# Conditioning weights in column halves, interleaved PSUM columns, the order of work at a stage seam, and a new share-out of routing one-hots in a decoder-layer kernel

## The chip, the cores and the metric

The kernel runs on one core of one Trainium2 chip. The metric is the device time of one execution in microseconds (us), taken as the median over repeated runs; lower is better. All times below are microseconds unless they are marked ns.

Engine names in the profile: PE is TensorE (PEld its weight loads), DVE is VectorE, ACT is ScalarE, POOL is GpSimd, SP is SyncE. A name with a q (SPq, ACTq, POOLq) is the instruction queue of that engine, where it issues transfers.

## The reference

One layer of a decoder on 1024 tokens of width 1024, all in float32:

```
mod = silu(c) @ ada_w + ada_b                    # (1024) @ (1024, 6144): six vectors
h   = rms_norm(x) * (1 + sc1) + sh1
... two kinds of causal attention on h, projected back ...
x   = x + g1 * (mixed @ w_out)
h2  = rms_norm(x) * (1 + sc2) + sh2
# PEER: 8 heads, 16 experts per head and token out of 128 * 128
q   = h2 @ w_q ; s = q . sub_keys                # two score lists of 128 per head
eidx, g = top-16 of the sums of the two lists' top-16, softmax
a   = gelu(u_tab[eidx] . h2)
y   = sum over the 128 chosen experts of g * a * v_tab[eidx]
x   = x + g2 * y
```

## The kernel before

The 1024 tokens are 8 tiles of 128. The program runs these stages one after another, and in each an engine takes its instructions in order:

1. **Conditioning and projections.** `ada(g, wp)` works out a third (2048 columns) of `mod`. The silu of c is repeated over 32 columns as the stationary operand, so one product fills only 32 of the 128 columns of TensorE's array, and four products for four blocks q of 512 columns can stand side by side (`tile_position=(0, 32 * q)`). For g = 0 a weight tile holds all four q (128x2048); for g = 1 and 2 it holds two of them (128x1024, contiguous rows of 4 KB), so each tile brings two products of 512 columns. These 32 tiles go through two buffers, issued by SP, and are woven into the projections (`project`), whose weights also come through SP.
2. **Attention, output projection and queries for tiles 0 to 4** (`block(0, DT)`).
3. **The same for tiles 5 to 7 (`block(DT, ...)`), woven with `route_dense`.** For each of tiles 0 to 4, `routing` finds the experts and `matrix(t)` turns them into a dense matrix of weights. It goes in 32 groups of four tokens: `A` holds for each token a one-hot row per chosen expert (VectorE, one instruction for four tokens), `B` a weighted one-hot row (one token at a time, on GpSimd, VectorE, or ScalarE, which needs two instructions, Abs and Relu). The string `SHARE[t]` says who does which of eight tokens: P, D or A. TensorE multiplies A by B, one product per token into a bank of PSUM `pg`; float32 products are two instructions each, so a group has eight. ScalarE (line 904) copies `pg` into `gs`, where the four tokens of a group lie next to each other and a row j begins every 32 elements. The copy reads PSUM in order and writes every 32nd element. Per tile this makes 128 B rows, 32 copies and 4 transfers `gd<-gs`. GpSimd also does the subtractions `wl` of the weight splits in this stage. The order on each engine in stages 1 to 3 is made by a planner that works from estimated costs.
4. **Experts** (`experts`, order written by hand). Step j of 128: `mm_u(j)`, 48 matmuls against two split tiles of the expert table, `us[2j]` and `us[2j+1]` (24 each); `gelu(j)`; `weigh(j)`, a product with the dense matrix; `split_c(j)`; and, from step 4 on, `mm_v` blocks that use `split_v` tiles. `split_u(n)` is a copy on ScalarE (high part), a subtraction (low part) on GpSimd where n < UP and else on VectorE, and the issue on SP of the load of tile n+3. `split_v(n)` is alike with VP. Between them `step()` runs a share of `gathered`: routing of tiles 5 to 7 and their gathered experts (VectorE multiplies at line 974, GpSimd issues the gathers at line 954).

The end of a step in stage 4, before:

```
if not blocks and live:          # j = 0 to 3
    for i in (j - 1, j) if j == NJ - 1 else (j - 1,):
        if i >= 0:
            weigh(i)
            if i < 2:
                split_c(i)
if jj % 2 == 1 and (g >= 0 or jj == 3):
    ...                          # two split_v
if live:
    split_u(2 * j + 3)
```

Of the kernel before, what the change touches and what calls it, by code (L numbers as in the profile page):

```python
# [24 lines left out]
P = 128  # L25
# [9 lines left out]
GB = 32  # L35
NA, NB = 3, 3
PACE = (1.3, 1.05, 1.5)
SHARE = ['PAPDPAPD', 'PAPDPAPD', 'PAPDPAPD', 'PDADPDAD', 'DDADPDAD']
NJ = 4
LAGS = 3  # L40
AHEAD = 2
PG = 2
LAGV = 2
UP, VP = 8, 8

UR, VR = 3, 4

# [38 lines left out]
def decoder_layer(ctx: ExitStack, tc: tile.TileContext, a, out):  # L86
# [8 lines left out]
    PS = {}  # L95
# [23 lines left out]
    def bank(name="pj"):  # L119
        return PS[name].tile([P, 512], FT, name=name)  # L120

    def tpt():
        return tp.tile([P, 4, P], FT, name="tp")
# [57 lines left out]
    def ada(g, wp):  # L181

        bt = wp.tile([P, 512], FT, name="abias", bufs=1)
        for q in range(4):
            o = a["ada_b"].offset + g * 2048 + q * 512
            (nc.gpsimd if g else nc.scalar).dma_start(bt[32 * q:32 * q + 32, :],
                                bass.AP(tensor=a["ada_b"].tensor, offset=o, ap=[[0, 32], [1, 512]]))
        ps = bank()
        n = 2 if g else 4
        for k in range(8):  # L190
            for q0 in range(0, 4, n):
                w = wp.tile([P, n, 512], FT, name="adaw")
                c = g * 2048 + q0 * 512
                (nc.sync if g or k % 2 == 0 else nc.scalar).dma_start(w, adaw[k, :, c:c + n * 512])
                for q in range(q0, q0 + n):
                    nc.tensor.matmul(ps[32 * q:32 * q + 32, :512], silb[:, k, :], w[:, q - q0, :], start=(k == 0),
                                     stop=(k == 7), skip_group_check=True, tile_position=(0, 32 * q))
        m = bt
        nc.vector.tensor_add(m, ps[:, :512], bt)
        for q in range(4 if g else 0):  # L200
            o = q * 512
            nc.gpsimd.dma_start(modd[2 * g + o // D, o % D:o % D + 512], m[32 * q:32 * q + 1, :])
        return m
# [661 lines left out]
    def route_dense(ts):  # L865

        with ExitStack() as c1:
            rp = pool(c1, "rp", 1)
            gp = pool(c1, "gp", 2)
            def matrix(t):  # L870
                r = R.pop(t)
                pt = tpt()
                for q in range(2):
                    nc.tensor.transpose(pt[:, q, :], r["e"][:, q, :], ident)
                nc.tensor.transpose(pt[:, 2, :], r["g"].rearrange("p h k -> p (h k)"), ident)
                T = gp.tile([P, 4, P], FT, name="T", bufs=1)
                nc.vector.tensor_copy(T[:, 0:3, :], pt[:, 0:3, :])  # L877
                nc.vector.tensor_scalar(T[:, 3, :], pt[:, 2, :], -1.0, None, op0=OP.mult)
                nj = gp.tile([P, P], FT, name="nj", bufs=1)
                nc.vector.tensor_scalar(nj, pt[:, 1, :], -1.0, None, op0=OP.mult)  # L880
                for b in range(P // GB):
                    gs = gp.tile([P, P, GB], FT, name="gs")
                    for m0 in range(0, GB, 4):
                        A = gp.tile([P, 4, P], FT, name="A", bufs=NA)
                        B = gp.tile([P, 4, P], FT, name="B", bufs=NB)
                        c = b * GB + m0
                        nc.vector.tensor_tensor(A, T[:, 0, c:c + 4, None].to_broadcast([P, 4, P]),
                                                iota128[:, None, :].to_broadcast([P, 4, P]), op=OP.is_equal)
                        for m in range(4):
                            who = SHARE[t][(m0 + m) % 8]  # L890
                            if who == "P":
                                nc.gpsimd.tensor_scalar(B[:, m, :], iota128, T[:, 1, c + m:c + m + 1],  # L892
                                                        T[:, 2, c + m:c + m + 1], op0=OP.is_equal, op1=OP.mult)
                            elif who == "A":
                                nc.scalar.activation(B[:, m, :], iota128, AF.Abs, bias=nj[:, c + m:c + m + 1])
                                nc.scalar.activation(B[:, m, :], B[:, m, :], AF.Relu, bias=T[:, 2, c + m:c + m + 1],
                                                     scale=T[:, 3, c + m:c + m + 1])
                            else:
                                nc.vector.tensor_scalar(B[:, m, :], iota128, T[:, 1, c + m:c + m + 1],
                                                        T[:, 2, c + m:c + m + 1], op0=OP.is_equal, op1=OP.mult)  # L900
                        pg = bank("pg").rearrange("p (a b) -> p a b", b=P) if "pg" in PS else tpt()
                        for o in range(4):
                            nc.tensor.matmul(pg[:, o, :], A[:, o, :], B[:, o, :], start=True, stop=True)  # L903
                        nc.scalar.activation(gs[:, :, m0:m0 + 4].rearrange("p j t -> p t j"), pg, AF.Copy)  # L904
                        yield 1.2
                    nc.scalar.dma_start(gd[:, :, t * (P // GB) + b].rearrange("p a j t -> p a (j t)"),
                                      gs.rearrange("p (a j) t -> p a (j t)", j=NJ))

            ts = list(ts)
            yield 10.0  # L910
            yield from routing(ts[0], rp)
            for t, nxt in zip(ts, ts[1:] + [None]):
                yield from weave((matrix(t), 1.0), (routing(nxt, rp) if nxt else iter(()), 0.8))
# [88 lines left out]
    def experts():  # L1002
        with ExitStack() as c1, tc.manual_schedule():
# [133 lines left out]
            for j in range(P + NJ):  # L1137
                if j == P:
                    tick(1.0)
                    fin["g2"] = rows(modd, 5 * D, D, gath.tile([P, D], FT, name="gath"), nc.sync)  # L1140
                    fin["x1"] = [gath.tile([P, D], FT, name="gath") for _ in range(DT)]
                    for i in range(DT):
                        nc.sync.dma_start(fin["x1"][i], x1d[i])
                    yr = yp.tile([P, 2, 512], FT, name="yr")
                    fin["rest"] = [yr[:, 0, :], yr[:, 1, :], gath.tile([P, D], FT, name="gath")[:, :512]]
                g, jj = j // NJ - 1, j % NJ
                blocks = [(g, c, i) for c, i in V[jj]] if g >= 0 else []
                live = j < P
                tk = [0]

                def step():
                    tk[0] += 1
                    tick((j + tk[0] / 6) / 127)

                if live:
                    ps = mm_u(j)
                if j == 0:
                    split_u(3)
                    for _ in range(10):
                        prog[0] = next(sg)  # L1160
                while pend:
                    retire()
                if jj == 0 and g >= 0:
                    split_c(j - 2)
                    split_c(j - 1)
                n0 = (2 * g + jj // 2) * NJ
                if g >= 0 and jj % 2 == 0:
                    split_v(n0 + 2)
                    split_v(n0 + 3)
                step()  # L1170
                if live:
                    split_u(2 * j + 2)
                step()
                if live:
                    gelu(j, ps)
                for b, blk in enumerate(blocks):
                    pv = mm_v(*blk)
                    if b == 0 and live:
                        weigh(j)
                        if jj < 2:  # L1180
                            split_c(j)
                    if len(pend) >= LAGV:
                        retire()
                    pend.append((*blk, pv))
                    step()
                if not blocks and live:

                    for i in (j - 1, j) if j == NJ - 1 else (j - 1,):
                        if i >= 0:
# [4 lines that stand above are left out]
                    n1 = (2 * g + jj // 2 + 1) * NJ  # L1194
                    split_v(n1)
                    split_v(n1 + 1)
                if live:
                    split_u(2 * j + 3)
                while tk[0] < 6:
                    step()  # L1200
# [92 lines left out]
```

## Time and profile before

| what | value |
|---|---|
| median of 3 runs | 3039.43 us (3036.16 to 3045.69) |
| the profiled execution | 3038.61 us, its span 3036.8 us |
| TensorE busy | 2837.1 us (93%) |
| VectorE busy | 2570.6 us (85%) |
| ScalarE busy | 1185.2 us (39%) |
| GpSimd busy | 1418.7 us (47%) |
| mean granted TensorE clock | 0.974 |

The span is the time from the first to the last instruction of the one profiled execution. Busy shares are averages over stages with different limits, so a stage has to be read by itself. TensorE's matmuls are pipelined, so that its busy time is above the time for which its array works.

### The profile page before, as it was taken

What the parts mean: (1) busy time and instruction counts of PE and PEld (TensorE: products, weight loads), DVE (VectorE), ACT (ScalarE), POOL (GpSimd) and SP (SyncE); (2) the same over time, 40 slices, a digit from 0 to 9 for tenths busy, and PEclk for the clock granted to TensorE, in tenths of its full rate; (3) what the DMA queues carried; (4) which work ended last, traced back from release to release, by engine and by line L of the source; (5) the groups of instructions that cost most, each with busy time, mean ns of one, the idle gap of its engine ahead of it and who ended that gap; (6) DMA issues with size and microseconds to landing.
All of it is one profiled execution on the core that took longest, in us unless ns stands there. A gap on an engine that the chain in (4) does not pass through costs nothing.

```text
span 3036.8 us, 46727 instructions
## 1 busy us (share of the span) xinstructions
PE 2837.1 (93%) x16323; PEld 2526.6 (83%) x16323; DVE 2570.6 (85%) x5380; ACT 1185.2 (39%) x2371; POOL 1418.7 (47%) x1194
## 2 busy tenths in 40 slices
PE   5999989897888799699999999999999999999998
PEld 3678777796776698699999999999989989998887
DVE  3767366599988899788888999999999999989997
ACT  4554375242886898222322222222222222222221
POOL 1121000000669974343444655566656666655761
PEclk9999999998999899899999999999999999999999
DMA  7664464721445664678798999899999999998995
GB/s 269 201 190 123 134 199 148 277 64 56 126 129 180 210 206 140 224 263 276 255 321 310 321 332 327 319 351 368 361 351 365 358 371 359 361 373 312 365 366 200
DMA packets 375564, 794.22 MB, mean 262 GB/s; under 512 B 31392, under 2 KB 171040, under 8 KB 368672
## 3 DMA queue, kind: packets, MB, share of 16 engines
q0 software_dynamic: 114400, 417.15, 38.3%
q1 hardware_dynamic: 153344, 312.48, 29.5%
q10 hardware_dynamic: 107584, 61.61, 6.9%
q8 instruction: 128, 2.10, 0.3%
q14 instruction: 108, 0.88, 0.1%
HBM read 707.74 MB, written 83.38 MB: 261 GB/s over the span
## 4 chain that ended last, share of the span: by engine, by line
PE 49%; DVE 18%; issue 12%; POOL 7%; DMA 6%; ACT 4%; SPq 0%; DVEq 0%; POOLq 0%; ACTq 0%
PE mm L1063 14%; PE pj L288 4%; PE pj L289 4%; PE pj L290 4%; POOL gath L954 4%; DVE yr L987 4%; DVE gath L974 3%; PE pg L903 3%; PE tp L289 2%; PE tp L290 2%; PE tp L288 2%; POOL B L892 2%; PE acc L288 1%; PE acc L289 1%; PE acc L290 1%
## 5 line engine op out<-in xcount | busy, mean ns | idle before, releaser
L1063 PE MATMUL mm<-h2d,uh 128*128 128x320 f32 x4096 | 770.6, 310 | 10.2 <-ACT C L1070 5.1
L954 POOL DMA_INDIRECT gath<-in_peer_u,ei x384 | 485.5, 1264 | 405.3 <-DVE gath L974 269.4
L1063 PEld LDWEIGHTS mm<-h2d,uh 128*128 128x128 f32 x4096 | 649.7, 189 | 21.1 <-ACT C L1070 6.2
L954 POOL DMA_INDIRECT gath<-in_peer_v,ef x384 | 514.9, 1341 | 307.2 <-DVE yr L987 168.7
L987 DVE SCALAR_TENSOR_TENSOR yr<-gath,co,yr 128x1024 f32<-128x1024 f32 x381 | 487.5, 1280 | 5.5 <-DMA gath<-in_peer_v,ef 1.1
L974 DVE SCALAR_TENSOR_TENSOR gath<-gath,h 128x1024 f32<-128x1024 f32 x384 | 462.7, 1221 | 26.0 <-DMA h<-h2d 13.4
L1063 PE MATMUL mm<-h2d,ul 128*128 128x320 f32 x2048 | 471.2, 311 | 12.9 <-DVE ul L279 12.4
L1070 ACT ACTIVATE C<-mm 128x640 f32<-128x640 f32 x128 | 90.5, 707 | 864.1 <-PE mm L1063 859.0
L892 POOL TENSOR_SCALAR B<-iota,T 128x128 f32<-128x128 f32 x240 | 265.6, 1115 | 266.5 <-DVE T L877 200.7
L1063 PEld LDWEIGHTS mm<-h2d,ul 128*128 128x128 f32 x2048 | 343.0, 188 | 18.3 <-DVE ul L279 17.9
L289 PE MATMUL tp<-vl,CH 128*128 128x512 f32 x600 | 235.6, 393 | 14.8 <-POOL vl L279 11.7
L903 PE MATMUL pg<-B,A 128*128 128x128 f32 x1280 | 197.2, 298 | 48.2 <-POOL B L892 26.8
L278 ACT ACTIVATE vh<-vr 128x512 fp32r<-128x512 f32 x256 | 152.9, 622 | 224.0 <-PE tp L290 145.5
L288 PE MATMUL tp<-vh,CH 128*128 128x512 f32 x600 | 234.6, 391 | 0.0
L290 PE MATMUL tp<-vh,CL 128*128 128x512 f32 x600 | 234.1, 390 | 0.0
L903 PEld LDWEIGHTS pg<-B,A 128*128 128x128 f32 x1280 | 174.9, 206 | 69.0 <-POOL B L892 39.3
L904 ACT ACTIVATE gs<-pg 128x512 f32<-128x512 f32 x160 | 173.8, 1087 | 56.7 <-PE pg L903 56.2
L278 ACT ACTIVATE uh<-ur 128x512 fp32r<-128x512 f32 x256 | 155.4, 619 | 74.8 <-DMA ur<-in_u_t 67.7
L279 DVE TENSOR_TENSOR ul<-ur,uh 128x512 fp32r<-128x512 f32 x248 | 173.6, 700 | 0.0
L279 DVE TENSOR_TENSOR vl<-vr,vh 128x512 fp32r<-128x512 f32 x248 | 160.0, 682 | 7.2 <-ACT vh L278 7.0
L1074 DVE TENSOR_TENSOR C<-C,G 128x640 f32<-128x640 f32 x128 | 105.2, 823 | 55.0 <-ACT C L1070 54.9
L288 PE MATMUL acc<-vh,CH 128*128 128x512 f32 x384 | 149.8, 390 | 0.0
(321 smaller groups left out, 5978.9 us busy)
## 6 DMA issues: line engine op xcount, KB each, us to landing
ur<-in_u_t SPq DMA_DIRECT2D x256, 256.0 KB, 6.3
vr<-in_peer_v SPq DMA_DIRECT2D x256, 256.0 KB, 6.9
gd<-gs ACTq DMA_DIRECT2D x20, 2048.0 KB, 9.3
G<-gd SPq DMA_DIRECT2D x32, 1280.0 KB, 8.8
adaw<-in_ada_w SPq DMA_DIRECT2D x32, 512.0 KB, 4.3
wraw<-in_peer_w_q SPq DMA_DIRECT2D x128, 128.0 KB, 2.7
wraw<-in_w_out SPq DMA_DIRECT2D x32, 256.0 KB, 3.6
wraw<-in_w_in SPq DMA_DIRECT2D x24, 256.0 KB, 3.8
```

The lines of the kernel that those rows point to most:

```text
L278: nc.scalar.activation(hi, src, AF.Copy)
L279: (eng or nc.vector).tensor_sub(lo, src, hi.bitcast(FT))
L288: nc.tensor.matmul(out, ah, bh, start=start, stop=False)
L289: nc.tensor.matmul(out, ah, bl, start=False, stop=False)
L290: nc.tensor.matmul(out, al, bh, start=False, stop=stop)
L892: nc.gpsimd.tensor_scalar(B[:, m, :], iota128, T[:, 1, c + m:c + m + 1], T[:, 2, c + m:c + m + 1], op0=OP.is_equal, op1=OP.mult)
L903: nc.tensor.matmul(pg[:, o, :], A[:, o, :], B[:, o, :], start=True, stop=True)
L904: nc.scalar.activation(gs[:, :, m0:m0 + 4].rearrange("p j t -> p t j"), pg, AF.Copy)
L954: nc.gpsimd.indirect_dma_start(out=u, out_offset=None, in_=tab, in_offset=bass.IndirectOffsetOnAxis(ap=idx, axis=0))
L974: nc.vector.scalar_tensor_tensor(got[n], got[n], 1.0, q["h2"], op0=OP.mult, op1=OP.mult, accum_out=q["dots"][:, s:s + 1])
L987: nc.vector.scalar_tensor_tensor(yr, v, q["co"][:, s:s + 1], yr, op0=OP.mult, op1=OP.add)
L1063: nc.tensor.matmul(ps[:, o, 0:C2], s[:, k % 4, :], h2[:, mv, k, o * C2:(o + 1) * C2], start=st, stop=(k == 7 and s is l))
```

## The change

Four things are edited.

- In `ada`, for g = 1 and 2, a weight tile holds 256 columns of each of the four blocks q instead of 512 columns of two of them. There are as many tiles of as many bytes. Each brings four products of 256 columns, side by side, into one of two PSUM banks (one per half of the columns); a row of a tile is four pieces of 1 KB. The bias is added in two halves. g = 0 keeps its sizes.
- In `matrix`, the product of token o goes to every fourth column of `pg`, so that `pg` is laid out (row j, token t). ScalarE's copy then reads PSUM in order and writes four neighbouring elements, then the next four 32 elements on.
- `SHARE`: per eight tokens one P becomes an A in tiles 0 to 2, and one D becomes an A in tiles 3 and 4: 80 rows B in all (48 off GpSimd, 32 off VectorE).
- In `experts`, `split_u(2j+3)` goes ahead of `weigh` and `split_c` in steps 1 to 3, `split_u(3)` goes from behind `mm_u(0)` to behind `gelu(0)`, and VP is 0, so that the subtractions of the first eight `split_v` go from GpSimd to VectorE.

```
-SHARE = ['PAPDPAPD', 'PAPDPAPD', 'PAPDPAPD', 'PDADPDAD', 'DDADPDAD']
+SHARE = ['PAADPAPD', 'PAADPAPD', 'PAADPAPD', 'PAADPDAD', 'DAADPDAD']
...
-UP, VP = 8, 8
+UP, VP = 8, 0
...
-        ps = bank()
-        n = 2 if g else 4
+
+        H = 256 if g else 512
+        pss = [bank() for _ in range(0, 512, H)]
         for k in range(8):
-            for q0 in range(0, 4, n):
-                w = wp.tile([P, n, 512], FT, name="adaw")
-                c = g * 2048 + q0 * 512
-                (nc.sync if g or k % 2 == 0 else nc.scalar).dma_start(w, adaw[k, :, c:c + n * 512])
-                for q in range(q0, q0 + n):
-                    nc.tensor.matmul(ps[32 * q:32 * q + 32, :512], silb[:, k, :], w[:, q - q0, :], start=(k == 0),
-                                     stop=(k == 7), skip_group_check=True, tile_position=(0, 32 * q))
+            for h0 in range(0, 512, H):
+                w = wp.tile([P, 4, H], FT, name="adaw")
+                src = adaw[k, :, g * 2048:(g + 1) * 2048].rearrange("p (q n) -> p q n", n=512)[:, :, h0:h0 + H]
+                (nc.sync if g or k % 2 == 0 else nc.scalar).dma_start(w, src)
+                for q in range(4):
+                    nc.tensor.matmul(pss[h0 // H][32 * q:32 * q + 32, :H], silb[:, k, :], w[:, q, :],
+                                     start=(k == 0), stop=(k == 7), skip_group_check=True, tile_position=(0, 32 * q))
         m = bt
-        nc.vector.tensor_add(m, ps[:, :512], bt)
+        for i, ps in enumerate(pss):
+            nc.vector.tensor_add(m[:, i * H:(i + 1) * H], ps[:, :H], bt[:, i * H:(i + 1) * H])
...
-                        pg = bank("pg").rearrange("p (a b) -> p a b", b=P) if "pg" in PS else tpt()
+
+                        pg = (bank("pg") if "pg" in PS else tpt().rearrange("p a b -> p (a b)")).rearrange(
+                            "p (j t) -> p j t", t=4)
                         for o in range(4):
-                            nc.tensor.matmul(pg[:, o, :], A[:, o, :], B[:, o, :], start=True, stop=True)
-                        nc.scalar.activation(gs[:, :, m0:m0 + 4].rearrange("p j t -> p t j"), pg, AF.Copy)
+                            nc.tensor.matmul(pg[:, :, o], A[:, o, :], B[:, o, :], start=True, stop=True)
+                        nc.scalar.activation(gs[:, :, m0:m0 + 4], pg, AF.Copy)
...
                 if j == 0:
-                    split_u(3)
                     for _ in range(10):
                         prog[0] = next(sg)
...
                 if not blocks and live:
+                    split_u(2 * j + 3)
 
                     for i in (j - 1, j) if j == NJ - 1 else (j - 1,):
```

## Rows read from the trace of the kernel before

**Rows 1.** The page's first part: busy us, share of the span, instructions.

```profile
span 3036.8 us, 46727 instructions
PE 2837.1 (93%) x16323; PEld 2526.6 (83%) x16323; DVE 2570.6 (85%) x5380; ACT 1185.2 (39%) x2371; POOL 1418.7 (47%) x1194
```

**Rows 2.** Busy time by stretch, one for each tile of `matrix`; clock, DMA share, GB/s last.

```profile
761.00:876.00 115.00, 101.67 (x717) 91.92 (x716) 101.72 (x278) 95.55 (x187) 74.96 (x70) 0.91 0.39 121
876.00:980.00 104.00, 82.98 (x498) 71.70 (x497) 92.33 (x227) 77.61 (x143) 93.41 (x78) 0.90 0.53 162
980.00:1064.00 84.00, 64.33 (x376) 54.93 (x374) 69.79 (x132) 66.51 (x128) 84.00 (x74) 0.90 0.67 217
1064.00:1135.00 71.00, 67.57 (x470) 65.36 (x471) 67.12 (x249) 65.36 (x143) 58.11 (x65) 0.98 0.66 201
1135.00:1213.00 78.00, 72.86 (x512) 68.91 (x510) 78.00 (x331) 64.52 (x139) 36.08 (x41) 1.00 0.50 146
```

**Rows 3.** The chain that ended last, 980 to 1064 us, shares by line.

```profile
by line: POOL B L892 50.7%; issue 13.1%; PE pg L903 11.4%; POOL wl L279 4.6%; PE pj L289 3.4%; PE pj L288 3.0%; PE pj L290 3.0%; DVE B L899 2.9%; ACT B L895 1.7%; DVE A L887 1.7%; ACT B L896 1.1%; PE tp L739 1.1%; ACT mH L278 0.7%; DVE T L8
```

**Rows 4.** Groups by form, 760 to 1215 us, and one of the page: busy us, mean ns | idle before.

```profile
L892 POOL TENSOR_SCALAR B<-iota,T 128x128 f32<-128x128 f32 x240 | 265.6, 1115 | 266.5 <-DVE T L877 200.7 <-PE pg L903 44.4 <-ACT B L896 5.1
...
L904 ACT ACTIVATE gs<-pg 128x512 f32<-128x512 f32 x160 | 173.8, 1087 | 56.7 <-PE pg L903 56.2 <-ACT sc L782 0.2
...
L899 DVE TENSOR_SCALAR B<-iota,T 128x128 f32<-128x128 f32 x240 | 92.9, 413 | 0.0
L896 ACT ACTIVATE B<-B,T 128x128 f32<-128x128 f32 x160 | 78.6, 495 | 7.6 <-ACT B L895 3.7 <-DMA h2d<-h2td 2.0 <-ACT sc L782 0.2
L895 ACT ACTIVATE B<-iota,nj 128x128 f32<-128x128 f32 x160 | 59.5, 374 | 0.6 <-DVE nj L880 0.6
...
L593 ACT ACTIVATE pT<-tp 128x512 f32<-128x512 f32 x26 | 15.6, 603 | 1.7 <-PE tp L592 1.7
...
L279 DVE TENSOR_TENSOR vl<-vr,vh 128x512 fp32r<-128x512 f32 x248 | 160.0, 682 | 7.2 <-ACT vh L278 7.0
```

**Rows 5.** The chain in order of time: start, us, what.

```profile
1110.51 0.90 PE pg L903 x8
...
1279.92 7.04 PE mm L1063 x48
```

**Rows 6.** Timeline of TensorE, conditioning: weight loads for g = 0, a tile for g = 1.

```profile
35.58 0.12 PEld L196 LDWEIGHTS pj<-adaw,silb 128*32 128x32 f32 x4 [0.31 <-issue]
36.01 0.12 PEld L196 LDWEIGHTS pj<-adaw,silb 128*32 128x32 f32 x4 [0.31 <-issue]
...
96.20 1.05 PE L196 MATMUL pj<-adaw,silb 128*32 128x512 f32 x4
97.19 0.45 PE L290 MATMUL pj<-wh,hL 128*128 128x384 f32 x1
```

**Rows 7.** The chain that ended last, 46 to 193 us, shares by line.

```profile
by line: PE pj L288 6.7%; DMA qd<-stage 6.6%; PE pj L289 6.0%; PE pj L290 5.9%; DMA wraw<-in_w_in 5.7%; PE pj L196 4.7%; DMA adaw<-in_ada_w 4.3%; PE tp L452 1.7%; issue 1.2%; ACT hf L367 1.1%; DVE stage L284 1.0%; DVE hf L370 0.8%; ACT hH L
```

**Rows 8.** Transfers: KB each, median us from issue to landing.

```profile
gd<-gs ACTq DMA_DIRECT2D x20, 2048.0 KB, 9.3
...
adaw<-in_ada_w SPq DMA_DIRECT2D x32, 512.0 KB, 4.3
```

**Rows 9.** Timelines of TensorE, VectorE and GpSimd at the seam to the experts.

```profile
1234.04 1.43 PE L1063 MATMUL mm<-h2d,uh 128*128 128x320 f32 x4 [5.06 <-ACT uh L278]
...
1273.71 0.80 PE L289 MATMUL tp<-vl,CH 128*128 128x512 f32 x1 [11.70 <-POOL vl L279]
...
1242.17 0.83 DVE L279 TENSOR_TENSOR CL<-C,CH 128x640 fp32r<-128x640 f32 x1 [2.92 <-ACT CH L278]
...
1267.43 1.22 DVE L974 SCALAR_TENSOR_TENSOR gath<-gath,h 128x1024 f32<-128x1024 f32 x1 [8.45 <-DMA gath<-in_peer_u,ei]
...
1269.85 1.55 DVE L279 TENSOR_TENSOR CL<-C,CH 128x640 fp32r<-128x640 f32 x2
...
1272.23 3.11 POOL L279 TENSOR_TENSOR vl<-vr,vh 128x512 fp32r<-128x512 f32 x2
```

## The prediction, made before the run

> **What bounds the kernel now.** I read the page first, for the span and the shares of the engines [rows 1]. TensorE is busy for 93%, but none of the edits takes work from the 1,750 us of the experts stage, which follows the seam, so the shares of the whole say little. What counts is the stretch in which each edit lies. So I cut the stage of `route_dense` into its five tiles and asked for the busy time of each engine in each [rows 2]. The reader should compare the largest number of a row with its length. In tile 2 GpSimd is busy for all 84.0 of 84 us; in tile 1 for 93.4 of 104, with VectorE close behind at 92.3. In tile 4 VectorE is busy for 78.0 of 78. In tile 3 VectorE, TensorE and ScalarE stand within 2.2 us of each other. In tile 0 nobody is full. The chain says the same for tile 2: half of it is rows B on GpSimd [rows 3]. Then the chain in the stretch of the conditioning [rows 7], which is a mixture: TensorE's projections, and transfers that come late. Last the timelines at the seam [rows 9]: TensorE stands idle twice, for 5.06 us and for 11.70 us.
>
> **The routing, costs.** The change takes 48 rows B from GpSimd, 16 in each of tiles 0 to 2, at 1.115 us [rows 4]: 17.8 us per tile. It takes 32 from VectorE, 16 in each of tiles 3 and 4, at 0.413: 6.6 us per tile. Each becomes two instructions on ScalarE, 0.374 + 0.495 = 0.869: 16 of them are 13.9 us per tile. ScalarE gets time back from the copy `gs`, 1.087 us now. The trace has no copy that writes runs of four elements. It has the same 512 elements of PSUM written in order, at 0.603 [rows 4], so the price lies between 0.603 and 1.087. If the excess of 0.484 us is owed to 512 jumps and the new copy has 128, it costs 0.603 + 0.121 = 0.724, and I take that: 32 copies of a tile are 11.6 us cheaper (15.5 to 0 at the bounds). So ScalarE's time per tile rises by 13.9 - 11.6 = 2.3 us (from -1.6 to +13.9).
>
> **The routing, by tile.** A tile takes at least the time of its busiest engine; the five take 1.13, 1.11, 1.00, 1.05 and 1.00 times that [rows 2].
> Tile 2: GpSimd falls from 84.0 to 66, VectorE at 69.8 is next, and with 1.05 of it the tile takes 73: -11 us.
> Tile 1: GpSimd falls from 93.4 to 75.6, but VectorE has 92.3; the tile keeps at least that, and I take 99: -5.
> Tile 4: VectorE falls from 78.0 to 71.4, TensorE has 72.9: -5.
> Tile 3: VectorE falls from 67.1 to 60.5, but TensorE has 67.6 and ScalarE comes to 67.7: -2.
> Tile 0: GpSimd was not the limit, ScalarE is 2.3 us fuller, yet each copy in the chain is shorter: -2.
> Together -25. If every relief came through until the next engine alone, it would be -11.7 in tile 1, -14.2 in tile 2 and -5 in tile 4 and some 10 in the other two: -41. If nothing but tile 2 gained, -10.
>
> **Every fourth column.** The trace has no matmul that writes PSUM with gaps. Below, it costs nothing: the eight instructions of a group take 0.90 us, 0.112 per 128 columns, while the split passes of the experts write 320 columns in 7.04/48 = 0.147 [rows 5]. A pass of `pg` thus writes a column every 0.88 ns where the other writes one every 0.46 ns. There is room for a write that is half as dense to take its own time. Above, I bound it by a doubling, 0.90 us for each of 160 groups, 144 us. A gain is excluded, since the same columns are streamed. I take nothing, as the nearest row shows TensorE writing columns at twice this rate; the upper bound is a rival below.
> [...]
>
> **The conditioning.** Of 48 weight tiles only the 32 of g = 1 and 2 change, and their bytes stay. A tile of two products of 512 columns keeps TensorE for 0.98 us from its start to the next instruction [rows 6]. Four products side by side are in the trace for g = 0: the weight loads of the last passes go out four together, one for each block q, 0.43 us after the four before. So four passes of 512 columns take 0.43 us, and the eight of a tile 0.86; four products take no more time than two do, which says that they run beside each other. With half the columns a tile would then take 0.43 to 0.55, which saves about 0.45 us, 14 us over 32 tiles. But conditioning is 4.7% of the chain of 147 us there, 6.9 us [rows 7], of which the half is 3.4; late transfers hold a sixth. So between -3 and -14, and I take -6, nearer the chain. Against it stand the pieces of 1 KB and the second bank. The transfers `gd<-gs` bring 4096 pieces of 512 bytes each in 9.3 us [rows 8]; a tile with 512 pieces of 1 KB, 4.3 us now, need not become slower. The two halves of the bias add are on no path, as `mod` is read again only after attention. SP's order and number of issues stay. If a held bank or a late tile stopped the projections, I allow +6.
>
> **The seam.** `mm_u(2)` needs `us[5]`. Its `split_u` is issued in step 1 behind `split_c(0)`, whose copy on ScalarE waits for `weigh(0)` on VectorE, so `uh[5]` comes late and TensorE waits 5.06 us [rows 9]. The change puts it ahead, and this wait goes. The load that it issues on SP (tile 8 in step 1, 10 and 12 after it) comes earlier too, in step 3 ahead of the matrix load that `weigh(3)` issues. Nothing of SP's work is pushed back except the load of tile 6, now issued behind `gelu(0)`, which is needed in step 2.
> `split_u(3)` now starts behind `gelu(0)`: a copy of about 0.6 us and a subtraction of about 1.6 [rows 4, 9]. `mm_u(1)` cannot start before `gelu(0)` anyway, and needs `us[3]` only for its second half, 24 x 0.147 = 3.5 us on [rows 5]. So this costs nothing; with the cover gone it would cost up to 2.2.
> What is late next is the wait of 11.70 us for `vl`. It hangs on VectorE: routing of tile 5, then 8.45 us for the first gathered rows, then two `CL`, then in GpSimd's queue, behind gathers, two `vl` [rows 9]. On that line VectorE loses the stall of 2.92 us (the copy it waited for stood behind `gelu(2)`) and gains two `vl` of 0.68 before the gathers [rows 4]: 1.6 us earlier. The next two `vl` then come on VectorE straight behind `CL`, some 1.6 us before GpSimd's first. That makes -3. The bounds are -8, if both waits shrink, and +5.5, if all eight subtractions, 8 x 0.682, lie on VectorE's path.
>
> **The sum.** -25 - 6 - 3 = -34 from the profiled execution's 3038.6 us, which is 0.8 under the median of the runs: 3005 us.
>
> **The rivals.**
> First, the copy gains nothing, because each jump on the way to SBUF costs and not only each single element: 1.087 as before. Then ScalarE has 13.9 us more per tile: 79.3 in tile 3, which took 71, and 78.4 in tile 4; +8 and 0, against -3 in tile 2 and -5 in tile 1: routing about 0, the whole -9, 3029 us. For it speaks that the write still has gaps; against it, that four elements share an address run.
> Second, and on the other side, TensorE slows with gaps in PSUM. Its idle time in the five tiles is 452 - 389.4 = 62.6 us [rows 2], which covers a factor of 1.43 on the 144 us of `pg`; beyond that TensorE is the bound and the routing relief is worth nothing. At a factor of 2 the stage grows by 144 - 62.6 = 81, and with -9 elsewhere the time is 3111 us (up to 3174 with no cover at all). For it speaks that writes with gaps are untested in this trace, against it the rates above. [...]
> Third, the relief is refilled: one engine's freed time becomes waiting for another in a stage where four are within a tenth of each other, and only tile 2 gains, -10. With -9 elsewhere: 3020 us.
> Fourth, every relief comes through: -41, -14, -8: 2976 us.
>
> **How the numbers follow.** The forecast, with 2985 to 3016 as its own range, has 0.60; the copy without gain 0.09; TensorE slowed 0.13; the refilled relief 0.12; all relief 0.06. The range reaches from 2978, near the fourth, over the third and the first to 3034, and leaves out the second and the tails of the others, about 2 in 10. About 0.3% (9 us) is what a measurement of this kernel can tell from no change. Faster takes the forecast, the fourth, nearly all of the third and half of the first, 0.78; the same 0.08; slower the second and mishaps of the seam, 0.14.
>
> **What would show it.** The copy at line 904's place near 0.72 us in place of 1.087; `pg` eight instructions still in about 0.90; GpSimd no longer full in the third tile, and that tile 11 us shorter; VectorE less than full in the fifth; a conditioning tile near 0.5 us; TensorE's wait for `uh` of 5.06 gone and its wait for `vl` shorter, with VectorE as the releaser. I would be wrong if `pg` matmuls stretch, if the planner orders the two woven stages in another way, or if VectorE, which gets nothing off in tiles 0 to 2, sets them all.

## The result and the profile after

The changed kernel takes 3011.14 us (median of 4 runs, 3009.56 to 3012.63) against 3042.07 us for the kernel before, run beside it: a ratio of 0.990, with a 95% interval of 0.9881 to 0.9919, or 31 us less. The forecast was 3005 us and 34 us less, with a range of 2978 to 3034.

The same stretches as in [rows 2], one for each tile of `matrix`, in the changed kernel (length; busy us of PE, PEld, DVE, ACT and POOL; clock, DMA share, GB/s):

```profile
763.00:877.00 114.00, 100.94 (x713) 90.68 (x714) 103.20 (x284) 95.33 (x222) 58.00 (x52) 0.93 0.40 122
877.00:985.00 108.00, 87.30 (x513) 76.36 (x512) 99.55 (x251) 76.33 (x175) 83.22 (x68) 0.91 0.52 156
985.00:1059.00 74.00, 58.90 (x382) 53.62 (x380) 66.37 (x153) 63.60 (x161) 66.85 (x59) 0.93 0.85 276
1059.00:1135.00 76.00, 73.75 (x529) 73.00 (x529) 67.29 (x263) 69.19 (x192) 62.68 (x71) 1.00 0.61 180
1135.00:1197.00 62.00, 57.73 (x429) 55.63 (x427) 61.93 (x270) 56.63 (x150) 27.30 (x28) 1.00 0.55 156
```

GpSimd no longer fills tile 2, which lost 10 us. VectorE's work in tile 4 fell with the tile, but it still fills it (61.93 of 62 us), against the sign that the forecast gave. Tile 0 is as long as it was, and tiles 1 and 3 are longer. Tile 2 is what the forecast said; the others are not.

The groups that answer to [rows 4] (busy us, mean ns of one | idle time before, and what ended it):

```profile
L894 POOL TENSOR_SCALAR B<-iota,T 128x128 f32<-128x128 f32 x192 | 222.5, 1165 | 310.9 <-DVE T L879 202.1 <-PE pg L907 64.5 <-ACT B L898 11.7
...
L898 ACT ACTIVATE B<-B,T 128x128 f32<-128x128 f32 x240 | 110.1, 490 | 5.2 <-DMA wraw<-in_peer_w_q 4.3 <-ACT sc L784 0.2
L908 ACT ACTIVATE gs<-pg 128x512 f32<-128x512 f32 x160 | 94.6, 592 | 40.8 <-PE pg L907 40.4
L897 ACT ACTIVATE B<-iota,nj 128x128 f32<-128x128 f32 x240 | 87.1, 397 | 3.4 <-DVE nj L882 3.3
L901 DVE TENSOR_SCALAR B<-iota,T 128x128 f32<-128x128 f32 x208 | 77.3, 390 | 0.0
```

The copy `gs` takes 0.592 us, no more than the copy that writes in order (0.603 [rows 4]). And TensorE, from the chain in order of time (start, us, what), answering to [rows 5]:

```profile
1071.65 0.89 PE pg L907 x8
```

The eight instructions of a group still take 0.89 us, with gaps of four columns between writes.

A conditioning tile on TensorE's timeline, answering to [rows 6]:

```profile
81.69 0.64 PE L197 MATMUL pj<-adaw,silb 128*32 128x256 f32 x8
82.26 0.39 PE L291 MATMUL pj<-wup,ql 128*128 128x256 f32 x1
```

From its start to the next instruction a tile takes 0.57 us where it took 0.98. The transfer of a tile, now in pieces of 1 KB, lands in 4.9 us at the median (4.3 in [rows 8]).

At the seam, VectorE's timeline (start, us, instruction, idle time before it) answers to [rows 9]:

```profile
1242.15 1.23 DVE L978 SCALAR_TENSOR_TENSOR gath<-gath,h 128x1024 f32<-128x1024 f32 x1 [7.13 <-DMA gath<-in_peer_u,ei]
...
1243.41 1.23 DVE L978 SCALAR_TENSOR_TENSOR gath<-gath,h 128x1024 f32<-128x1024 f32 x1
...
1244.56 1.55 DVE L281 TENSOR_TENSOR CL<-C,CH 128x640 fp32r<-128x640 f32 x2
1246.03 1.29 DVE L281 TENSOR_TENSOR vl<-vr,vh 128x512 fp32r<-128x512 f32 x2
```

and TensorE's waits there, in total:

```profile
PE tp L291 <- DVE vl L281: 10.3, 1, 10.3
PE mm L1067 <- ACT C L1074: 5.6, 4, 3.3
PE mm L1067 <- DVE ul L281: 1.1, 1, 1.1
PE mm L1067 <- POOL ul L281: 0.3, 1, 0.3
```

The wait of 5.06 us for `uh` is gone, and the wait for `vl` has VectorE as its releaser.

One profile of this kernel can be off by several us in a stretch that no edit touches (up to 4 in the table by tile below), so below a stretch is read from all kernels that share its edits. The kernel before itself ran between 3031 and 3053 us over the study, and within one kernel the longer runs tend to have the lower mean granted TensorE clock (`e4_seam` below: 3025.82 us at 0.977, 3045.14 us at 0.969). Differences in us are a ratio's distance from 1 times 3040.

### The profile page after: what moved, and what is told of

Same layout as the page of the kernel before. It is cut to its first block, busy times and chain, and to the rows that moved or that the text cites. A ratio compares the mean times of both kernels' runs of the same rounds, so it can differ in the third digit from the quotient of the medians.

```text
span 3010.8 us, 47052 instructions
## 1 busy us (share of the span) xinstructions
PE 2817.1 (94%) x16451; PEld 2528.1 (84%) x16451; DVE 2553.0 (85%) x5358; ACT 1179.4 (39%) x2531; POOL 1357.1 (45%) x1138
## 4 chain that ended last, share of the span: by engine, by line
PE 39%; DVE 15%; issue 9%; DMA 4%; ACT 3%; POOL 3%; SPq 0%; DVEq 0%; ACTq 0%; POOLq 0%
PE mm L1067 16%; DVE yr L991 5%; PE tp L291 3%; PE tp L292 3%; PE tp L290 3%; PE pg L907 2%; DVE gath L978 2%; PE pj L291 2%; PE pj L292 2%; PE pj L290 2%; POOL gath L958 2%; PE acc L290 2%; PE acc L291 2%; PE acc L292 2%; DVE vl L281 1%
## 5 line engine op out<-in xcount | busy, mean ns | idle before, releaser
L894 POOL TENSOR_SCALAR B<-iota,T 128x128 f32<-128x128 f32 x192 | 222.5, 1165 | 310.9 <-DVE T L879 202.1
L907 PE MATMUL pg<-B,A 128*128 128x128 f32 x1280 | 187.4, 293 | 31.9 <-POOL B L894 16.3
L291 PE MATMUL acc<-vl,CH 128*128 128x512 f32 x384 | 149.7, 390 | 0.0
```

The source lines that it names most:

```text
L291: nc.tensor.matmul(out, ah, bl, start=False, stop=False)
L907: nc.tensor.matmul(pg[:, :, o], A[:, o, :], B[:, o, :], start=True, stop=True)
```

## The experiments

**The four parts, each alone on the kernel before.** Conditioning in halves (`e1_cond`):

```
-        n = 2 if g else 4
+        H = 256 if g else 512
+        pss = [bank() for _ in range(0, 512, H)]
...
-                w = wp.tile([P, n, 512], FT, name="adaw")
+                w = wp.tile([P, 4, H], FT, name="adaw")
```

> Conditioning in halves alone, on the kernel before. In the changed kernel the last transposes of the projections come 5.0 us earlier (342.3 to 337.3 us), but the first transposes of h2 (541.7 us before) come at 542.0. Theory A: the stretch between, attention of tiles 0 to 4, gives the gain back by itself, so here too the projections end 5 us earlier, nothing is left at the h2 transposes, and the time is that of before within 0.15% (3037 to 3047). Rival B: the loss in attention came from the other edits through the planner, and this edit alone keeps its 5 to 6 us (about 3036, ratio 0.998).

Measured: 3032.24 us, ratio 0.9967 (0.9955 to 0.998), 10 us less. Theory A falls as far as the time goes: the edit keeps its gain, and the 10 us are more than the 5 to 6 of rival B.

Every fourth column (`e2_columns`):

```
-                            nc.tensor.matmul(pg[:, o, :], A[:, o, :], B[:, o, :], start=True, stop=True)
-                        nc.scalar.activation(gs[:, :, m0:m0 + 4].rearrange("p j t -> p t j"), pg, AF.Copy)
+                            nc.tensor.matmul(pg[:, :, o], A[:, o, :], B[:, o, :], start=True, stop=True)
+                        nc.scalar.activation(gs[:, :, m0:m0 + 4], pg, AF.Copy)
```

> Every fourth PSUM column alone, on the kernel before. Theory A: the copy gs falls to about 0.59 us and the eight pg instructions of a group stay at 0.90 us, so ScalarE gets 79 us back, but it limits none of the five tiles: GpSimd still fills the third tile (84 us) and VectorE the fifth; gain 3 to 8 us, ratio 0.997 to 0.999. Rival B: ScalarE's copy is what paces the groups, one pg bank after another, and this edit carries most of the change: 15 us or more, ratio 0.995 or less. Rival C (PSUM with gaps slows the matmul): pg passes stretch beyond 0.112 us each and the time rises.

Measured: 3027.98 us, ratio 0.9956 (0.994 to 0.9972), 13 us less, between theories A and B. The order of instructions is on every engine that of the kernel before, so the two kernels differ only in the copy and in where the columns of `pg` lie; the `pg` instructions still start 0.112 us apart, so rival C falls. The first tile, busy time by engine as above:

```profile
762.80:865.70 102.90, 93.66 (x710) 84.25 (x709) 99.43 (x274) 84.61 (x186) 75.02 (x70) 1.00 0.44 133
```

It takes 102.9 us where it took 115 [rows 2], though ScalarE was not full before (95.55). The other four tiles hardly moved (the table below). In the first tile ScalarE's queue also holds the attention's exponentials, and only one bank of `pg` is there (`pg=1` in `attend`, two banks later), so a shorter copy can come back as time. The chain that ended last in this tile, shares by line, before and with the columns, agrees: the copy `gs` has 8.0% of it, then 3.1%.

```profile
by line: PE pg L903 24.9%; PE mm L580 18.2%; PE ov L659 11.5%; ACT gs L904 8.0%; issue 7.4%; PE tp L592 4.2%; ACT pT L593 3.0%; ACT p L564 2.4%; ACT L564 2.2%; ACT B L896 2.1%; ACT pd L564 2.0%; ACT pm L564 1.9%; ACT B L895 1.7%; DVE A L887
...
by line: PE mm L580 17.6%; PE pg L905 13.8%; PE ov L659 10.0%; DVE A L887 7.4%; DVE nm L558 4.7%; PE tp L592 4.2%; ACT pT L593 3.8%; DVE B L899 3.2%; ACT gs L906 3.1%; issue 2.8%; ACT pd L564 2.6%; DVE oh L838 2.4%; ACT B L896 2.3%; ACT pm 
```

Not all of the 12 us is the copy's. The granted TensorE clock of the tile was 0.91 before and is 1.00 here; 0.91 is a mean: in the kernel before the clock was 0.50 from 779.3 to 786.1 us and from 827.2 to 840.7, about a fifth of the tile, and 1.00 in the rest. The seam kernel below (`e4_seam`) runs the instructions of the kernel before up to its seam, and had 0.98 in this tile:

```profile
762.40:873.10 110.70, 96.02 (x715) 86.53 (x714) 100.92 (x277) 95.15 (x187) 73.84 (x70) 0.98 0.41 124
```

So some 4 us of the 12 go with the clock and some 8 with the copy. From 820 to 830 us, where the clock fell in the kernel before (0.86 on average), TensorE was busy for 6.81 us; with the columns, where it did not fall there, for 6.98. Why it fell in the one and not in the other is open.

The share-out (`e3_share`), with the copy as it was:

```
-SHARE = ['PAPDPAPD', 'PAPDPAPD', 'PAPDPAPD', 'PDADPDAD', 'DDADPDAD']
+SHARE = ['PAADPAPD', 'PAADPAPD', 'PAADPAPD', 'PAADPDAD', 'DAADPDAD']
```

> The new share-out of rows B alone, with the copy gs still at about 1.09 us. Theory A: GpSimd's relief works without the cheaper copy in the third tile (about -11 us there), but ScalarE, 13.9 us fuller per tile, binds in the fourth and fifth; total gain 0 to 10 us, ratio 0.997 to 1.000. Rival B: GpSimd and VectorE are the limit throughout, ScalarE has room, and this edit alone brings 20 us or more, ratio below 0.994.

Measured: 3045.38 us, ratio 1.0019 (1.0006 to 1.0032): 6 us slower, worse than theory A's range, and rival B falls. Without the cheaper copy the share-out costs.

The seam (`e4_seam`):

```
-UP, VP = 8, 8
+UP, VP = 8, 0
...
                 if j == 0:
-                    split_u(3)
...
                 if not blocks and live:
+                    split_u(2 * j + 3)
```

> Seam order and VP = 0 alone, on the kernel before. In the changed kernel the stretch from the last gs transfer to the first gather index of tile 5 fell from 45.7 to 37.5 us. Theory A (the step of the prediction): the order itself is worth about 3 us, since VectorE's routing of tile 5 sets the end of the seam; the other 5 us came from VectorE being ahead when the routing of tile 5 begins. Ratio about 0.999. Rival B: the order is worth all 8 us, ratio about 0.997.

Measured: 3027.38 us, ratio 0.9965 (0.9949 to 0.998), 11 us less. By the time that is rival B; two runs below take the order and VP = 0 apart.

**Columns and share-out together (`e5_columns_share`), and everything but the share-out (`e9_no_share`).** The edits are the second and third of those above, and all but the third.

> Every fourth column and the new share-out together, without conditioning and seam. Theory A: the share-out is paid for by the cheaper copy; alone it cost about 6 us (1.0019), with ScalarE's 79 us back it is worth the 25 us of the prediction's routing sum together with the columns, ratio 0.992. Theory B: columns alone gave 13 us (0.9956), and the share-out takes some of it back, because what it wins in the third and fifth tiles it loses in the other three: ratio 0.995 to 0.997.

> The changed kernel with the share-out undone (conditioning, columns and seam stay). Single parts measured -10, -13 and -11 us, sum -34. Theory A (the share-out is needed to use the cheaper copy): slower than the changed kernel's 3011 us by 8 us or more. Theory B (it is worth nothing or costs): 3005 to 3012 us, ratio 0.988 to 0.990.

Measured: 3021.75 us, ratio 0.9936 (0.9915 to 0.9957), and 3014.18 us, ratio 0.9915 (0.9889 to 0.994). Together the two routing edits bring 19 us, 6 more than the columns alone, where the intervals overlap, and the changed kernel (0.990) is ahead of the one without the share-out by an amount inside both intervals. Both results lie between their two theories, and neither decides. So the share-out as a whole is worth little. By tile it is not: this table has the time of each tile, from the start of the first tile's `T` copy, or the fourth transfer `gd<-gs` of the tile before, to its own fourth transfer, one profile each.

```
kernel                     tile 0   tile 1   tile 2   tile 3   tile 4    sum
before                      114.6    103.8     84.7     70.6     78.1   451.8
conditioning                113.6    109.0     83.5     75.5     71.7   453.3
seam                        110.7    100.7     84.4     73.3     77.8   446.9
share-out                   122.4    108.8     77.3     80.4     72.9   461.8
columns                     102.9    100.2     85.4     70.6     78.4   437.5
columns, share-out          114.0    100.4     72.5     72.5     75.0   434.4
all but share-out           102.7    105.2     82.9     76.0     70.5   437.3
all (the changed kernel)    113.5    108.4     73.3     76.4     62.3   433.9
```

Read down the columns, with two cautions. The first and the third row have the same instructions in tiles 0 to 3 and differ by up to 4 us there, so a step of that size shows nothing. And the conditioning, which touches no instruction of `matrix`, moves tiles 1, 3 and 4 by +5, +5 and -6, as the planner orders the later stages in another way with it. In tile 0 the new share-out costs 8 us with the old copy and 11 with the new, and takes back what the columns gave; of the 11, some 3 to 4 may be the clock, an estimate from the 4 us above, as it was 1.00 without the new share-out and 0.93 or 0.94 with it. In tile 2 it gives 7 to 13. In tile 3 it costs 10 with the old copy and nothing clear with the new. In tile 4 it gives 3 to 8.

**The share-out where it helps (`e10_share_24`).** The changed kernel with

```
+SHARE = ['PAPDPAPD', 'PAPDPAPD', 'PAADPAPD', 'PDADPDAD', 'DAADPDAD']
```

> The changed kernel with the new share-out in the third and fifth tiles only, the old one in the other three. In the traces, tiles with the columns alone took 103, 100, 85, 71 and 78 us, and in the changed kernel 114, 108, 73, 76 and 62. Theory B (a tile's share-out acts in that tile): 103 + 100 + 73 + 71 + 62 = 409 us in place of 434, so some 25 us faster than the changed kernel, about 2986 us, ratio 0.982. Theory A (tile times follow from how the two woven streams stand to each other, and a tile's gain is the next one's loss): within 8 us of the changed kernel, 3003 to 3015.

Measured: 2998.25 us, ratio 0.9856 (0.9829 to 0.9883). That is 13 us below the changed kernel, half of what theory B hoped for, with intervals that just touch, and 16 us below the median of the kernel without the share-out (`e9_no_share`), clear of its interval. Busy time by tile, as above:

```profile
760.70:863.40 102.70, 94.62 (x718) 85.88 (x719) 99.62 (x275) 85.61 (x188) 74.84 (x70) 1.00 0.46 134
863.40:969.00 105.60, 84.90 (x498) 72.39 (x497) 96.44 (x236) 65.75 (x142) 99.52 (x81) 0.90 0.52 160
969.00:1043.20 74.20, 60.35 (x386) 54.39 (x386) 68.05 (x159) 63.28 (x159) 63.81 (x59) 0.93 0.85 274
1043.20:1122.80 79.60, 75.69 (x536) 73.86 (x535) 76.16 (x291) 60.63 (x162) 62.57 (x72) 1.00 0.58 170
1122.80:1186.20 63.40, 57.94 (x427) 55.71 (x425) 63.30 (x272) 56.22 (x150) 27.84 (x29) 1.00 0.54 156
```

Tiles 0, 2 and 4 came out as hoped (103, 73 and 62 expected), tiles 1 and 3 at 105.6 and 79.6 where 100 and 71 were expected. But 100 and 71 come from a kernel without the conditioning. The row with all but the share-out has 105.2 and 76.0 there, and with these theory B's sum is 102.7 + 105.2 + 73.3 + 76.0 + 62.3 = 419.5 us in place of 433.9: 14 us less, near the 13 measured. The profile shows 425.5, 8 less. So the time agrees with a share-out that acts in its own tile, and most of the miss is the wrong base.

**One more step (`e11_first_two`).** From there,

```
+SHARE = ['PAPPPAPD', 'PAPAPAPD', 'PAADPAPD', 'PDADPDAD', 'DAADPDAD']
```

> The share-out of the fastest version so far (new in the third and fifth tiles), and one of eight rows B goes from VectorE to GpSimd in the first tile and from VectorE to ScalarE in the second. In that version VectorE is busy for 99.6 of the first tile's 102.7 us (GpSimd 74.8, ScalarE 85.6) and for 96.4 of the second's 105.6 (GpSimd 99.5, ScalarE 65.8). Theory B (the fullest engine of a tile sets it): the first tile loses 4 to 5 us; the second, where GpSimd is full as well, at most 3; about 2992 us, ratio 0.983 to 0.985. Theory A (the two streams only shift): no change within 0.2%, ratio 0.985 to 0.988, or slower.

Measured: 3003.99 us, ratio 0.9884 (0.9864 to 0.9905). Not faster, and theory B's rule misses here. In tile 0 GpSimd's busy time rose by 13.7 us, VectorE's fell by 0.6 only, though 16 rows B left it, and the tile stayed at 102 us:

```profile
758.00:860.40 102.40, 93.84 (x702) 85.17 (x703) 99.03 (x270) 83.86 (x184) 88.55 (x83) 0.98 0.45 135
```

Tiles 2 to 4 have the same rows B as in `e10_share_24`, and took 70.6, 74.2 and 72.4 us here against 74.2, 79.6 and 63.4 there, 217.2 in both. So a tile's time depends on its neighbours too, as theory A has it, and a gain of one tile counts only when the whole time shows it.

**The seam in two.** The order alone (`e6_order`: the move of the two `split_u` lines, VP = 8) and VP = 0 alone (`e7_vp`):

> The new place of split_u(2j+3) and split_u(3) alone, VP still 8. The seam alone gave about 11 us. Theory A: the order is what gives it: the wait of 5.06 us for uh goes and the routing of tile 5 on VectorE ends earlier; ratio 0.997. Theory B: the order gives the 3 us that the prediction put on it (0.999), and the rest came from VP = 0, which takes the two vl out of GpSimd's queue behind the gathers (the wait of 11.70 us).

> VP = 0 alone, split_u where it was. Seam and VP together measured 0.9965, the order alone 0.9994. Theory A: VP = 0 carries the rest, since the two vl no longer stand in GpSimd's queue behind gathers: ratio 0.996 to 0.998, and TensorE's wait for vl of 11.70 us is shorter while that of 5.06 us for uh stays. Rival B: neither is worth much alone and only the two together shorten the seam: ratio 0.999 to 1.000.

Measured: 3035.99 us, ratio 0.9994 (0.9978 to 1.0009), and 3033.69 us, ratio 0.9981 (0.9968 to 0.9994): 2 and 6 us, to 11 for both. TensorE's waits at the seam, in total, in the kernel before:

```profile
PE tp L289 <- POOL vl L279: 11.7, 1, 11.7
PE mm L1063 <- ACT C L1070: 5.1, 4, 2.8
PE mm L1063 <- ACT uh L278: 5.1, 1, 5.1
PE mm L1063 <- DVE ul L279: 2.9, 2, 1.7
```

with the order alone:

```profile
PE tp L289 <- POOL vl L279: 10.2, 1, 10.2
PE mm L1063 <- ACT C L1070: 6.6, 4, 2.7
PE mm L1063 <- DVE ul L279: 4.3, 1, 4.3
```

and with VP = 0 alone:

```profile
PE tp L289 <- DVE vl L279: 8.6, 1, 8.6
PE mm L1063 <- ACT uh L278: 6.6, 1, 6.6
PE mm L1063 <- ACT C L1070: 5.1, 4, 2.7
PE mm L1063 <- DVE ul L279: 1.9, 2, 1.4
```

The order removes the wait for `uh`, but the waits for `ul` and for `C` grow by 1.4 and 1.5 us, and the one for `vl` falls by 1.5: in all 24.8 us become 21.1. VP = 0 brings the wait for `vl` from 11.7 to 8.6 us and keeps the wait for `uh`: 22.2 in all. With both, in the changed kernel, it is 17.3. From the last transfer `gd<-gs` to the end of the span the traces have 1823.8 us before, 1819.8 with the order, 1819.0 with VP = 0, and 1813.6 to 1816.3 in the five float32 kernels with both (1820.0 and 1817.6 in the two bfloat16 ones below). The four other kernels with neither have 1819.9 to 1825.0, so these traces show the two together, and neither alone. By the times theory B fits the order, which is worth the 2 to 3 us of the prediction or nothing (its interval holds 1), and theory A fits VP = 0. But the two intervals overlap, and that of VP = 0 reaches into rival B's range: which of the two gives more is not shown.

**Gaps at the faster rate.** The changed kernel with `A` and `B` in bfloat16 (`e12_half_gaps`), and the same with contiguous `pg` columns and the old copy (`e13_half_row`):

```
-                        A = gp.tile([P, 4, P], FT, name="A", bufs=NA)
-                        B = gp.tile([P, 4, P], FT, name="B", bufs=NB)
+                        A = gp.tile([P, 4, P], BF, name="A", bufs=NA)
+                        B = gp.tile([P, 4, P], BF, name="B", bufs=NB)
```

> The changed kernel with A and B kept in bfloat16, so that B's weights are rounded, and one instruction per product in place of two; pg still written to every fourth column. In float32 a pass of 128 columns takes 0.111 us, with gaps or without. Theory A: the gap costs nothing because a float32 pass writes a column only every 0.87 ns; a bfloat16 pass that writes at twice the rate is slowed by the gaps, so a group of four takes longer here than with contiguous columns. Rival B: gaps cost nothing at this rate either, and four products take the same time in both.

> The same with contiguous columns in pg and the old copy to gs (A and B in bfloat16, B rounded). The pair is read for the time of the four products of a group alone: Theory A has it shorter than with gaps, rival B the same.

TensorE's timeline with gaps, groups of one and of four products that ran through:

```profile
1083.48 0.28 PE L907 MATMUL pg<-B,A 128*128 128x128 bf16 x1
...
1105.45 0.60 PE L907 MATMUL pg<-B,A 128*128 128x128 bf16 x4
1106.24 0.61 PE L907 MATMUL pg<-B,A 128*128 128x128 bf16 x4
```

and with contiguous columns:

```profile
1105.89 0.40 PE L905 MATMUL pg<-B,A 128*128 128x128 bf16 x4
1107.23 0.23 PE L905 MATMUL pg<-B,A 128*128 128x128 bf16 x1
```

A further product of 128 columns takes (0.60 - 0.28)/3 = 0.107 us with gaps and (0.40 - 0.23)/3 = 0.057 without. Theory A: here a write with gaps takes TensorE 0.107/128 us, or 0.83 ns, a column, and a float32 pass of 0.111 us per 128 columns is slow enough to hide it. In a slower stretch of the same two traces, with gaps and without, a group takes

```profile
824.15 1.06 PE L907 MATMUL pg<-B,A 128*128 128x128 bf16 x4
...
822.99 0.63 PE L905 MATMUL pg<-B,A 128*128 128x128 bf16 x4
```

and there the third and fourth products start 0.213 us after the one before with gaps, 0.107 without. So the price of a gap is no fixed time: it is 0.050 us a product above and 0.106 here, where a product without gaps takes 0.107 in place of 0.057. A group of eight float32 passes takes 2.05 us without gaps where the granted clock was 0.50 (the kernel before, at 831.62 us) and 2.05 with them (the changed kernel, at 829.99 us, also at 0.50), 0.214 and 0.213 us a pass: there too the gap costs it nothing. The whole times, 2999.97 and 3023.53 us, are one run each and no comparison of the columns.

## Why the prediction was right, point by point

- **The sum** was right, its terms less so. Routing was to give 25 and gave 19 (columns and share-out together, 13 to 26); conditioning 6, and 10 (6 to 14) alone; the seam 3, and 11 (6 to 16) alone. These add up to 40, and the whole gave 30 (25 to 36): parts overlap, or the intervals hide it. That 34 came so near is partly luck: the routing was put too high, the seam and the conditioning too low.
- **Every fourth column** was costed at nothing for TensorE, by the rate of the float32 passes. Right, and the pair in bfloat16 shows the reason: the gap would have doubled a pass at twice the rate. Gaps slow the bfloat16 products (0.107 against 0.057 us) and not the float32 products (0.89 us per eight with gaps, 0.90 without). So the second rival falls for this kernel.
- **The copy** was taken at 0.724 us, as if each jump cost the same; it takes 0.592. Four neighbours are as good as 512, so the term was mis-sized by 0.13 us a copy; the measured copy lies below the lower bound of 0.603. A jump after every element costs (1.087 us against 0.603), one after every fourth does not (0.592); why is not shown. The first rival falls with it.
- **The routing by tile** is the step that failed, though its sum held within the interval. By the table the tiles 0 to 4 changed by -1, +5, -11, +6 and -16 us; the forecast was -2, -5, -11, -2 and -5. Tile 2 was right, and GpSimd there went from full to 66.85 us. Tiles 1 and 3 grew and tile 4 fell by three times its forecast, a good part of which goes with the conditioning, whose effect on the order of the later stages the prediction named as a way to be wrong but did not price: without it (the row of columns and share-out) they are at -3, +2 and -3. Tile 0 was put at -2, with ScalarE a little fuller and each copy shorter. It has two effects of some 8 us each, and 11 to 12 with the clock, that cancel: the shorter copy gives, the 16 rows B on ScalarE take. The rule that a tile takes the time of its fullest engine does not see them. That ScalarE is there a station in a chain, through one bank of `pg` and the softmax, is what the chain's shares suggest; no run changed the number of banks. The third rival (only tile 2 gains) is nearest to what happened to the share-out; tile 4 also gained.
- **The conditioning**: the tile was to take 0.43 to 0.55 us and takes 0.57. That the column blocks run side by side is shown: eight passes of 256 columns, at 0.111 us per 128, would take 1.78 us one after another. The last transposes of the projections come at 337.7 us on average in the five float32 kernels with halves and at 343.5 in seven without, 5.8 us earlier, and 6 was forecast for the whole. At the start of `route_dense` the means are 760.1 and 761.2, so most of it is lost in attention and the first queries, while the time alone shows 10. Where those 10 come back is open: the planner also orders the later stages in another way with this edit, and one profile of it (3038.58 us) is longer than the median. The prediction's 48 weight tiles are 40; the 32 that change were right.
- **The seam**: the wait for `uh` went, and the wait for `vl` has VectorE as releaser, as said. The size was off: 3 forecast, 11 measured alone, some 7 in the traces (1822.6 us on average in the five kernels with neither edit, 1815.3 in the five with both). The order was worth about what the whole step was put at; the term for VP = 0, 1.6 us of gain against 1.4 of loss, was too small by the 6 us (2 to 10) that it measured alone.

## What to carry to other kernels

Before changing who does what in a stage where four engines are near full, write the busy time of each by stretch and change only the stretches where the engine to be relieved is the fullest and the receiving one has room: the same share-out cost 8 to 11 us in tile 0 and gave 7 to 13 in tile 2, and keeping it in two tiles of five gave 2998 us, against 3011 in all five and 3014 in none. Then measure, as the next such step gave nothing. Before a stretch of one profile is compared with another's, compare their granted clocks: of two kernels with the same instructions there, one took 114.6 us in a tile at 0.91 and the other 110.7 at 0.98. When a transposing copy is slow, move the jump to the side that has time to spare: here TensorE's float32 writes, whose rate hides a gap (0.89 us per eight passes with gaps, 0.90 without), took it from ScalarE at no cost.

## What the runs showed of the hardware

- ScalarE's copy of 128x512 float32 from PSUM takes 0.603 us written in order, 0.592 in runs of four with 128 bytes from run to run, and 1.087 with every element 128 bytes from the next.
- TensorE's writes to every fourth column of PSUM cost nothing for float32 products (0.111 us per pass of 128 columns either way, and 0.214 without and 0.213 with gaps where the granted clock was 0.50) and about double a bfloat16 product (0.107 against 0.057 us, and 0.213 against 0.107 in a slower stretch of the same two traces).
- Four float32 products of 32 rows and 256 columns in four column blocks of the array take 0.57 us, two of 512 columns in two blocks 0.98 us, for the same bytes of weights.
